# Second block's attention: two partition halves in one item, score products in turn, value products turned round

## The chip, the cores and the metric

One Trainium2 chip, and of its eight cores one. The metric is the device time of one execution of the program in microseconds; the kernel before ran three times for it, and one further execution was taken by the hardware profiler.

## The reference, cut to what matters

Two blocks of two layers each work on 256 tokens of width 1024. The change touches the attention of the second block, which each of its two layers computes twice: once with a window and a sink (kind 0 in the kernel, two shared key and value heads), once causal over one block of 256 keys (kind 1, eight heads each for q, k and v).

```python
HEAD_DIM = 64
def hybrid_layer_2(x, c, positions, ...):
    h = adaln(rms_norm(x, g_mix), sh1, sc1)
    proj = h @ w_in
    q_a, k_a, v_a, q_b, k_b, v_b, gate_a, gate_b = jnp.split(proj, IN_OFFSETS, axis=-1)
    ...
    y_a = swa_attention(q_a, k_a, v_a, sinks) @ w_o_swa
    y_b = moba_attention(q_b, k_b, v_b) @ w_o_moba
    mixed = jax.nn.sigmoid(gate_a) * y_a + jax.nn.sigmoid(gate_b) * y_b
    x = x + gt1[:, None, :] * (mixed @ w_out)

def swa_attention(q, k, v, sinks):
    s = einsum(q, k) * HEAD_DIM ** -0.5        # window of 128 keys: a query block of 128 sees at most 256
    p = softmax(concatenate([where(valid, s, NEG_INF), sink]))[..., :-1]
    return einsum(p, v)

def moba_attention(q, k, v):                   # 256 tokens are one block, so its own block is all there is
    ...
    s_own = where(kpos <= qpos, einsum(qc, k_own) * scale, NEG_INF)
    return einsum(softmax(s_own), v_own)
```

## The kernel before, in words

All large products are streams of weight tiles. A tile of 128 x 1024 float32 comes by DMA, ScalarE rounds it to a high part (`w<-w` on ACT), VectorE makes the low part as the difference (`w<-w,w` on DVE), and TensorE does three products a tile and output: high by high, high by low, low by high, in the one-pass format fp32r. A tile of a product with token rows out is twelve matmuls of 512 columns (`mm<-w,h`), one with features out twenty-four of 256 (`mm<-h,w`). At most three tiles are split ahead of TensorE.

Everything else is written as items: generators that issue a few instructions and yield what they wait for. A planner keeps a model of each engine's time (`Planner.note` adds the cost of each instruction) and decides after each weight step which item goes on, so the order on each engine comes out of that model. Attention items run in four lanes; a lane has two 128 x 512 tiles, named a and b (`l0a`, `l0b`, ... , and `vb` twice for the fourth lane), and a tile of small columns (`ls`). Four PSUM banks named p are shared by all items.

An attention item before is `group(t, hg)`: query block `t` of 128 tokens, and heads of one parity `e_`, whose q and k lie in partitions 0 to 63 or 64 to 127 of `qk`. For `t` = 0 there are two groups of four heads with 128 keys, for `t` = 1 four groups of two heads with 256 keys, so six a kind. A group does: score products with 64 rows of contraction into one bank (`p<-s`, 64*128 in the profile), mask add, row maximum, exponentials with their sums on ScalarE, four transposes (`p<-cst,l0a` and so on), a copy back to the lane's tile b, value products with the weights of the attention as the stationary side (128 x 128) and 64 columns of v moving (`p<-s,l1b` and so on), and a multiplication by the reciprocal of the sum into a tile `av`. When the groups of a block `t` are done, `outp` transposes `av` four times (`p<-cst,s`) and splits the result into high and low parts in `oo`. These attention products are plain float32 and stand in the profile as two records each; a transpose is one.

Kind 0 is set going when the third weight group of a layer's projections (q of kind 1) is done, and runs beside the products for k and v of kind 1; kind 1 follows beside the four gate products, and `oo` is used after those.

Of the kernel before, what the change touches and what calls it, by code (L numbers as in the profile page):

```python
# [7 lines left out]
F32 = mybir.dt.float32  # L8
F32R = mybir.dt.float32r
I32 = mybir.dt.int32  # L10
AF = mybir.ActivationFunctionType
# [74 lines left out]
class Planner:  # L86
# [46 lines left out]
    def note(self, eng, op, args, kw):  # L133
# [7 lines left out]
        if eng == PE:  # L141
# [441 lines left out]
def _build(tc, a, out, es):  # L583
# [22 lines left out]

    def LS(lane):

        t = sm.tile([128, 20], F32, name=f"ls{lane}", tag=f"ls{lane}")
        off = [0]  # L610

        def take(n):
            off[0] += n
            return t[:, off[0] - n:off[0]]
        return take
# [1351 lines left out]
        yield [sc2]  # L1967
        yield from rows2(0)

    def attend_items(kind, qk, vv, oo, avs, scol, need):  # L1970
        def group(t, hg, av):
            def gen(lane):
                yield [plan.after(g) for g in need]
                msk, rw, sc_ = B["msk"], B["rw"], LS(lane)
                nk = t + 1
                hpb = 4 // nk
                n = 128 * nk
# [3 lines left out]
                e_, p0 = hg % 2, hpb * (hg // 2)  # L1981
                gs_ = [2 * (p0 + i) + e_ for i in range(hpb)]
                gsl = slice(gs_[0], gs_[-1] + 1, 2)
                rr = slice(64 * e_, 64 * e_ + 64)
# [9 lines left out]
                sv = s.rearrange("p (h n) -> p h n", n=n)  # L1994
                nc.vector.tensor_tensor(sv, Sv, mk, ALU.add)
                plan.release(S)
                yield [s]
                mx = sc_(4)[:, 0:hpb]
                nc.vector.tensor_reduce(mx, sv, AX.X, ALU.max)
                yield [mx]  # L2000
                cs = scol[kind, t][:, gsl]
                sk, nsk = (b[:, gs_[0]:gs_[-1] + 1:2] for b in (rw[:, 256:264], B["nsk"]))
                nb = sc_(4)[:, 0:hpb]
                nc.vector.scalar_tensor_tensor(nb, mx, -1.0, cs, ALU.mult, ALU.mult)
                yield [nb]
                if kind == 0:
                    nc.vector.tensor_tensor(nb, nb, nsk, ALU.min)
                    yield [nb]
                    es_ = sc_(4)[:, 0:hpb]
                    nc.vector.tensor_tensor(es_, sk, nb, ALU.add)  # L2010
                den = sc_(4)[:, 0:hpb]
                for i in range(hpb):
                    nc.scalar.activation(sv[:, i, :], sv[:, i, :], AF.Exp, bias=nb[:, i:i + 1], scale=cs[:, i:i + 1],
                                         accum_out=den[:, i:i + 1])
                if kind == 0:
                    nc.scalar.activation(es_, es_, AF.Exp)
                yield [s, den]
# [12 lines left out]
                for i in range(hpb):  # L2030
                    g = gs_[i]
                    vo = 128 + 64 * g if kind else 64 * (g % 2)
                    for k in range(nk):
                        b = i * nk + k
# [4 lines left out]
                if kind:  # L2039
                    d = av.rearrange("p (h e d) -> p e h d", e=2, d=64)[:, e_, p0:p0 + hpb, :]  # L2040
                else:
                    d = av.rearrange("p (e h d) -> p e h d", e=2, d=64)[:, e_, p0:p0 + hpb, :]
                nc.vector.tensor_tensor(d, o_[:, 0:64 * hpb].rearrange("p (h d) -> p h d", d=64),
                                        rd.unsqueeze(2).to_broadcast([128, hpb, 64]), ALU.mult)
                plan.release(o_)
            return gen

        def outp(t, av, name):
            def gen(_):
                yield [plan.after(name)]  # L2050
                pt = yield Bank(av)
                transposes(pt, av, 4)
                yield [pt]
                ts = slice(128 * t, 128 * t + 128)
                yield from split(oo[:, kind, 0, :, ts], oo[:, kind, 1, :, ts], pt.rearrange("p (i n) -> p i n", n=128))
                plan.release(pt)
            return gen
        for t in range(2):
            name = f"att{kind}{t}"
            for hg in range(2 * (t + 1)):  # L2060
                plan.add(name, group(t, hg, avs(t)))
            plan.add(f"att{kind}", outp(t, avs(t), name), kind="pri")

    def residual(gt, c, X, sv, on_token):
        cs = slice(512 * c, 512 * c + 512)
# [14 lines left out]
    def layer2(l, X, norm, begin_next, on_token):  # L2080
# [7 lines left out]
        def pre_a():  # L2088
            st["qk"] = slot("s2", [128, 16, 256])
            t = slot("s3", [128, 4096])  # L2090
            st["vv"] = t[:, 0:1280].rearrange("p (t n) -> p t n", t=2)
            st["av"] = t[:, 1280:3328].rearrange("p (i n) -> p i n", i=4)

        def trans(qr, nb, dst, t):
            pt = yield Bank(qr)
# [26 lines left out]
        def attend(kind):  # L2122
            if not kind:
                if not l:
                    stream.gone()
                st["oo"] = slot("s4", [128, 2, 2, 4, 256], F32R)
            attend_items(kind, st["qk"], st["vv"], st["oo"], lambda t: st["av"][:, 2 * kind + t, :], scol,
                         (f"qk{kind}",))
# [294 lines left out]
```

## Time and profile before

| what | us |
|---|---|
| three runs | 2275.04, 2276.93, 2282.97 |
| median | 2276.93 |
| profiled execution, its own time | 2281.12 |
| its span, first to last instruction | 2278.6 |
| TensorE busy in the span | 2235.9 |
| VectorE, ScalarE, GpSimd busy | 1491.5, 1108.1, 268.7 |

The span is what the trace's rows add up to; the profiled execution's own time has 2.5 us around it. A busy TensorE is one with some matmul in flight, and since matmuls overlap, what a matmul costs is read from the distance between the starts of neighbours, not from its duration.

### The profile page before, as it was taken

What the parts mean: (1) busy time and instruction counts of PE and PEld (TensorE: products, weight loads), DVE (VectorE), ACT (ScalarE), POOL (GpSimd) and SP (SyncE); (2) the same over time, 40 slices, a digit from 0 to 9 for tenths busy, and PEclk for the clock granted to TensorE, in tenths of its full rate; (3) what the DMA queues carried; (4) which work ended last, traced back from release to release, by engine and by line L of the source; (5) the groups of instructions that cost most, each with busy time, mean ns of one, the idle gap of its engine ahead of it and who ended that gap; (6) DMA issues with size and microseconds to landing.
All of it is one profiled execution on the core that took longest, in us unless ns stands there. A gap on an engine that the chain in (4) does not pass through costs nothing. (4 is left out here: it accounts for less than half of the span.)

```text
span 2278.6 us, 34907 instructions
## 1 busy us (share of the span) xinstructions
PE 2235.9 (98%) x13192; PEld 1894.9 (83%) x13192; DVE 1491.5 (65%) x2868; ACT 1108.1 (49%) x2140; POOL 268.7 (12%) x451
## 2 busy tenths in 40 slices
PE   8999999999999999999999999999999999999999
PEld 6877888877777877878898888997998987798987
DVE  4767745567676635676885867678666656758554
ACT  4345323245465423435543566556655645656653
POOL 1013000033121000110200332002000002100000
PEclk9999999999999999999999999999999999999999
DMA  7443443443323454365683423464354564346454
GB/s 296 147 156 103 138 158 130 153 162 102 111 93 103 152 180 142 134 204 175 224 277 134 153 88 121 162 206 148 103 193 161 185 212 158 111 140 211 151 193 148
DMA packets 99912, 359.84 MB, mean 158 GB/s; under 512 B 11960, under 2 KB 12272, under 8 KB 99744
## 3 DMA queue, kind: packets, MB, share of 16 engines
q1 hardware_dynamic: 96192, 348.34, 45.6%
q0 software_dynamic: 3552, 9.28, 1.6%
q8 instruction: 103, 1.69, 0.3%
q14 instruction: 65, 0.53, 0.1%
HBM read 354.37 MB, written 3.20 MB: 157 GB/s over the span
## 5 line engine op out<-in xcount | busy, mean ns | idle before, releaser
L318 PE MATMUL mm<-h,w 128*128 128x256 f32 (+1 forms) x4048 | 819.7, 320 | 2.1 <-ACT qr L318 1.0
L318 DVE TENSOR_TENSOR w<-w,w 128x1024 fp32r<-128x1024 f32 x452 | 552.7, 1223 | 391.0 <-ACT w L318 340.8
L318 ACT ACTIVATE w<-w 128x1024 fp32r<-128x1024 f32 x461 | 486.4, 1058 | 661.9 <-PE mm L318 605.2
L318 PEld LDWEIGHTS mm<-h,w 128*128 128x128 f32 x4048 | 602.8, 190 | 61.6 <-issue 13.8
L318 PE MATMUL mm<-w,h 128*128 128x512 f32 (+1 forms) x1584 | 474.4, 394 | 10.8 <-DVE w L318 7.6
L318 PE MATMUL mm<-hl,w 128*128 128x512 f32 (+1 forms) x1040 | 354.2, 341 | 0.0
L318 PEld LDWEIGHTS mm<-w,h 128*128 128x128 f32 x1584 | 287.6, 191 | 79.8 <-DVE w L318 12.1
L318 PE MATMUL mm<-s,w 128*128 128x256 f32 (+1 forms) x1536 | 254.1, 325 | 1.1 <-DVE s L318 0.6
L318 PEld LDWEIGHTS mm<-s,w 128*128 128x128 f32 x1536 | 223.1, 190 | 25.3 <-issue 3.2
L318 PE MATMUL mm<-w,s 128*128 128x512 f32 x996 | 240.1, 391 | 0.0
L318 PE MATMUL mm<-w,hl 128*128 128x512 f32 (+1 forms) x608 | 232.9, 383 | 0.0
L318 PEld LDWEIGHTS mm<-w,s 128*128 128x128 f32 x996 | 186.2, 188 | 38.5 <-issue 0.4
L318 PEld LDWEIGHTS mm<-hl,w 128*128 128x128 f32 x1040 | 197.4, 190 | 20.8 <-issue 2.9
L318 DVE SCALAR_TENSOR_TENSOR acc<-w,stat,acc 128x512 f32<-128x512 f32 x192 | 143.8, 749 | 44.6 <-DMA w<-in_wada_dram 37.7
L318 PEld LDWEIGHTS mm<-w,hl 128*128 128x128 f32 x608 | 115.7, 190 | 22.6 <-DVE hl L318 0.2
L318 ACT ACTIVATE s<-mm 128x512 f32<-128x512 f32 (+2 forms) x142 | 67.2, 480 | 63.9 <-PE mm L318 63.7
L318 PE MATMUL p<-s 64*128 64x256 f32 (+3 forms) x464 | 85.8, 390 | 3.0 <-DVE s L318 1.5
L318 POOL TENSOR_TENSOR qrs<-qrs,mhalf 128x8 f32<-128x8 f32 (+2 forms) x48 | 80.2, 1672 | 4.0
L318 POOL TENSOR_SCALAR ls<-ls 128x1 f32<-128x1 f32 x72 | 25.9, 360 | 398.3 <-ACT l0a L318 124.7
L318 PE MATMUL mm<-s,s 128*128 128x512 f32 x252 | 67.8, 390 | 0.0
L318 PEld LDWEIGHTS p<-s 64*128 64x128 f32 (+1 forms) x464 | 47.0, 186 | 23.5 <-issue 6.3
L318 DVE TENSOR_REDUCE ls<-p 128x1 f32<-128x512 f32 (+1 forms) x96 | 52.9, 594 | 12.4 <-PE p L318 12.2
(314 smaller groups left out, 2422.2 us busy)
## 6 DMA issues: line engine op xcount, KB each, us to landing
w<-in_win_dram SPq DMA_DIRECT2D x272, 512.0 KB, 3.5
w<-in_wada_dram SPq DMA_DIRECT2D x144, 512.0 KB, 3.8
w<-in_wmix_dram SPq DMA_DIRECT2D x64, 512.0 KB, 3.6
w<-in_wup_dram SPq DMA_DIRECT2D x64, 512.0 KB, 3.7
w<-in_wdn_dram SPq DMA_DIRECT2D x64, 512.0 KB, 4.3
w<-in_wo_dram SPq DMA_DIRECT2D x16, 512.0 KB, 3.5
w<-in_wout_dram SPq DMA_DIRECT2D x16, 512.0 KB, 3.7
s<-in_x_dram SPq DMA_DIRECT2D x4, 512.0 KB, 8.0
```

What stands on the lines that cost most here:

```text
L318: r = f(*a, **k)
```

## The change

An item is now `group(t, p0)` and holds both partition halves: one item a kind for `t` = 0 (eight heads), two for `t` = 1 (four heads each), so three a kind in place of six. It takes two banks at once and issues its score products in turn, one of the lower and one of the upper half. It uses tiles a and b of its lane for the two halves, and small columns of eight, with the sink's term in columns of its own. The weights of the attention are multiplied by the reciprocal before they are transposed (two VectorE operations of 512 columns an item), the transposed weights go back into the same tiles, and the value products are turned round: v is the stationary side (128 rows, 64 columns), the weights move with 128 columns, and the two products of a pair write partitions 0 to 63 and 64 to 127 of one bank. The result lies as `oo` wants it, so `av` and `outp` go. The planner counts a matmul with 64 rows out, and a float32 one with 64 rows of contraction, at half.

```diff
-            if not f32 and ins[0].shape[0] == 64:
+            if ins[0].shape[0] == 64 or out.shape[0] == 64:
                 c /= 2
...
-        t = sm.tile([128, 20], F32, name=f"ls{lane}", tag=f"ls{lane}")
+        t = sm.tile([128, 24], F32, name=f"ls{lane}", tag=f"ls{lane}")
...
-                S = yield Bank(qk)
-                Sv = S.rearrange("p (h n) -> p h n", n=n)
+                gsl = slice(2 * p0, 2 * p0 + 2 * hpb)
+                heads = lambda x, e: x[:, e::2]
+                S = yield Bank(qk, n=2)
                 for i in range(hpb):
-                    g = gs_[i]
-                    kk = 12 if kind == 0 else 8 + g // 2
-                    nc.tensor.matmul(Sv[:, i, :], qk[rr, 4 * kind + g // 2, 128 * t:128 * t + 128], qk[rr, kk, 0:n],
-                                     start=True, stop=True)
-                yield [S]
-                s = LT(lane, "a")
...
+                    for e in range(2):
+                        rr = slice(64 * e, 64 * e + 64)
+                        kk = 12 if kind == 0 else 8 + p0 + i
+                        nc.tensor.matmul(S[e][:, n * i:n * i + n], qk[rr, 4 * kind + p0 + i, 128 * t:128 * t + 128],
+                                         qk[rr, kk, 0:n], start=True, stop=True)
+                yield S
+                s = [LT(lane, w) for w in "ab"]
...
-                rd = sc_(4)[:, 0:hpb]
-                nc.vector.reciprocal(rd, den)
-                pt = yield Bank(s)
-                transposes(pt, s, 4)
-                yield [pt]
-                wt = LT(lane, "b")
-                nc.scalar.activation(wt, pt, AF.Copy)
-                plan.release(pt)
-                o_ = yield Bank(wt)
...
-                        nc.tensor.matmul(o_[:, 64 * i:64 * i + 64], wt[:, 128 * b:128 * b + 128], vv[:, k, vo:vo + 64],
-                                         start=(k == 0), stop=(k == nk - 1))
+                nc.vector.reciprocal(den, den)
+                for e in range(2):
+                    yield [den]
+                    nc.vector.tensor_tensor(sv[e], sv[e], heads(den, e).unsqueeze(2).to_broadcast([128, hpb, n]), ALU.mult)
+                for e in range(2):
+                    pt = yield Bank(s[e])
+                    transposes(pt, s[e], 4)
+                    yield [pt]
+                    nc.scalar.activation(s[e], pt, AF.Copy)
+                    plan.release(pt)
+                o_ = yield Bank(*s)
+
+                if kind:
+                    visits = [(i, [(e, i) for e in range(2)]) for i in range(hpb)]
+                else:
+                    visits = [(e * hpb // 2 + i, [(e, 2 * i + m) for m in range(2)]) for i in range(hpb // 2)
+                              for e in range(2)]
+                for blk, pair in visits:
                     for k in range(nk):
...
+                        for m, (e, i) in enumerate(pair):
+                            vo = 128 + 64 * (2 * (p0 + i) + e) if kind else 64 * e
+                            b = i * nk + k
+                            nc.tensor.matmul(o_[64 * m:64 * m + 64, 128 * blk:128 * blk + 128], vv[:, k, vo:vo + 64],
+                                             s[e][:, 128 * b:128 * b + 128], start=(k == 0), stop=(k == nk - 1))
                 yield [o_]
...
-                nc.vector.tensor_tensor(d, o_[:, 0:64 * hpb].rearrange("p (h d) -> p h d", d=64),
-                                        rd.unsqueeze(2).to_broadcast([128, hpb, 64]), ALU.mult)
+                ts = slice(128 * t, 128 * t + 128)
+                ks = slice(p0, p0 + hpb) if kind else slice(p0 // 2, 4, 2) if t else slice(0, 4)
+                yield from split(oo[:, kind, 0, ks, ts], oo[:, kind, 1, ks, ts],
+                                 o_[:, 0:128 * hpb].rearrange("p (i n) -> p i n", n=128))
...
-        def outp(t, av, name):
-            def gen(_):
-                yield [plan.after(name)]
-                pt = yield Bank(av)
-                transposes(pt, av, 4)
```

The order on TensorE where the first score products of the first layer stand (`s_14757` is `qk`; `-` is the kernel before, `+` the changed one):

```order
 L318 MATMUL mm<-w_15068,h 128x512
-L318 MATMUL p_15110<-s_14757 128x128 x4
+L318 MATMUL p_15110<-s_14757 128x128
+L318 MATMUL p_15111<-s_14757 128x128
+L318 MATMUL p_15110<-s_14757 128x128
+L318 MATMUL p_15111<-s_14757 128x128
+L318 MATMUL p_15110<-s_14757 128x128
+L318 MATMUL p_15111<-s_14757 128x128
+L318 MATMUL p_15110<-s_14757 128x128
+L318 MATMUL p_15111<-s_14757 128x128
 L318 MATMUL mm<-w_15068,h 128x512
```

The four products of the second group, which stood one half tile further down, have moved up between the first four, and the two banks alternate.

TensorE in the kernel before, kind 0 of the same layer, between the fifth and the sixth tile after those scores (`s_14758` holds v):

```order
L318 MATMUL p_15314<-cst,l2a 128x128 x4
L318 MATMUL p_15321<-cst,vb_15234 128x128 x4
L318 MATMUL p_15332<-cst,l0a 128x128 x4
L318 MATMUL p_15341<-s_14758,l1b 128x64 x4
L318 MATMUL p_15359<-s_14757 128x256 x2
L318 MATMUL p_15365<-s_14758,l2b 128x64 x4
L318 MATMUL p_15370<-s_14758,vb_15328 128x64 x4
L318 MATMUL mm<-w_15296,h 128x512
```

and in the changed kernel the value products and a transpose of the same kind and layer:

```order
L318 MATMUL p_15552<-l2a,s_14758 64x128 x4
L318 MATMUL p_15552<-l2b,s_14758 64x128 x4
L318 MATMUL p_15562<-cst,vb_15307 128x128 x4
L318 MATMUL p_15570<-s_14757 128x256
L318 MATMUL p_15571<-s_14757 128x256
L318 MATMUL p_15570<-s_14757 128x256
L318 MATMUL p_15571<-s_14757 128x256
L318 MATMUL mm<-h,w_15500 128x256 x2
```

The transposes and value products of kind 0, which stood beside the products for v of kind 1 (`mm<-w,h`), now stand beside the first gate product (`mm<-h,w`), eight to eleven tiles after the first scores; the output has 64 rows and 128 columns.

VectorE of the changed kernel in the second layer, five to six weight tiles after the first scores (`w_18863` and `w_18918` are low parts of weight tiles, `vb` are score tiles of one item, `qr`, `g` and `ssq` belong to the projections):

```order
L318 TENSOR_TENSOR w_18863<-w_18684,w_18849 128x1024
L318 TENSOR_TENSOR g<-qr,hl 128x512
L318 TENSOR_TENSOR qr<-qr,hl 128x512
L318 TENSOR_TENSOR qr<-qr,g 128x512
L318 TENSOR_REDUCE ssq<-g 128x8
L318 TENSOR_TENSOR vb_18907<-p_18811,hl 128x512
L318 TENSOR_TENSOR vb_18908<-p_18812,hl 128x512
L318 SCALAR_TENSOR_TENSOR ls_18728<-ls_18728,scol 128x4
L318 TENSOR_TENSOR qr<-qr,qrs 128x512
L318 TENSOR_TENSOR g<-qr,hl 128x512
L318 TENSOR_TENSOR qr<-qr,hl 128x512
L318 TENSOR_TENSOR w_18918<-w_18735,w_18883 128x1024
```

Before, the fullest stretch between two low parts there held eight operations of 512 columns, one of 256 and eight small ones; now it holds nine of 512 and one small one. TensorE's order is the same outside the stretches with attention, but for eight transposes that move by a few matmuls; SyncE's and GpSimd's are the same throughout.

## Rows read from the trace of the kernel before

**Rows 1.** The page, busy time of each engine: us, share of the span, instructions.

```profile
PE 2235.9 (98%) x13192; PEld 1894.9 (83%) x13192; DVE 1491.5 (65%) x2868; ACT 1108.1 (49%) x2140; POOL 268.7 (12%) x451
```

**Rows 2.** Windows: length, busy (count) of PE, PEld, DVE, ACT, POOL, PEclk, DMA.

```profile
1573.00:1661.00 88.00, 87.00 (x605) 77.61 (x605) 59.46 (x119) 56.27 (x128) 9.77 (x10) 1.00 0.35 114
```

**Rows 3.** Groups by shape, TensorE, 1573 to 1661: count, busy us, mean ns, idle before.

```profile
L318 PE MATMUL p<-s 64*128 64x256 f32 x32 | 7.9, 402 | 0.5 <-DVE s L318 0.5
...
L318 PE MATMUL p<-s,l2b 128*128 128x64 f32 x24 | 3.3, 279 | 0.0
...
L318 PE MATMUL p<-cst,s 128*128 128x128 f32 x16 | 2.4, 272 | 0.0
```

**Rows 4.** Timeline of TensorE, score products: start us, length us, records, idle before.

```profile
1574.72 1.16 PE L318 MATMUL p<-s 64*128 64x128 f32 x8
1575.81 1.66 PE L318 MATMUL mm<-w,h 128*128 128x512 f32 x6
...
1581.87 1.14 PE L318 MATMUL p<-s 64*128 64x256 f32 x8
1582.94 0.96 PE L318 MATMUL mm<-w,h 128*128 128x512 f32 x3
```

**Rows 5.** Timeline of TensorE, value products and transposes after them.

```profile
1598.48 1.13 PE L318 MATMUL p<-s 64*128 64x256 f32 x4 [0.52 <-DVE s L318]
1599.54 1.10 PE L318 MATMUL p<-s,l2b 128*128 128x64 f32 x8
1600.48 1.06 PE L318 MATMUL p<-s,vb 128*128 128x64 f32 x8
1601.35 3.02 PE L318 MATMUL mm<-w,h 128*128 128x512 f32 x12
1604.21 0.60 PE L318 MATMUL p<-cst,s 128*128 128x128 f32 x4
1604.57 0.71 PE L318 MATMUL mm<-w,h 128*128 128x512 f32 x2
```

**Rows 6.** Timeline of TensorE, four column groups of 32 at a time.

```profile
1312.98 0.43 PE L318 MATMUL p<-acc,one 128*32 128x128 f32 x8
1313.34 0.39 PE L318 MATMUL mm<-h,w 128*128 128x256 f32 x1
```

**Rows 7.** Timeline of VectorE, second layer, where kind 0 begins.

```profile
1938.28 1.23 DVE L318 TENSOR_TENSOR w<-w,w 128x1024 fp32r<-128x1024 f32 x1 [1.50 <-ACT w L318]
1940.07 0.69 DVE L318 TENSOR_REDUCE ssq<-g 128x8 f32<-128x512 f32 x1 [0.56 <-ACT g L318]
...
1942.86 1.22 DVE L318 TENSOR_TENSOR w<-w,w 128x1024 fp32r<-128x1024 f32 x1
1943.99 0.68 DVE L318 TENSOR_REDUCE ssq<-g 128x8 f32<-128x512 f32 x1
1944.59 0.68 DVE L318 TENSOR_TENSOR vb<-p,hl 128x512 f32<-128x512 f32 x1
```

**Rows 8.** Timeline of TensorE at the same place.

```profile
1941.39 1.16 PE L318 MATMUL p<-s 64*128 64x128 f32 x8
```

**Rows 9.** Timeline of VectorE, second layer, waits behind TensorE.

```profile
1957.41 0.42 DVE L318 TENSOR_TENSOR s<-p,ls 128x256 f32<-128x256 f32 x1 [0.99 <-PE p L318]
...
1961.29 0.69 DVE L318 TENSOR_TENSOR vb<-p,hl 128x512 f32<-128x512 f32 x1 [1.12 <-PE p L318]
```

**Rows 10.** Timeline of TensorE, waits for a weight tile's low part.

```profile
1018.17 0.50 PE L318 MATMUL mm<-w,h 128*128 128x512 f32 x1 [1.77 <-DVE w L318]
...
1590.30 0.97 PE L318 MATMUL mm<-w,h 128*128 128x512 f32 x3 [0.48 <-DVE w L318]
...
1964.49 2.07 PE L318 MATMUL mm<-w,h 128*128 128x512 f32 x4 [2.43 <-DVE w L318]
```

**Rows 11.** Windows behind two of these waits, columns as in rows 2.

```profile
1018.00:1032.00 14.00, 13.83 (x45) 9.49 (x46) 4.47 (x13) 1.78 (x2) 0.00 (x0) 0.53 0.25 91
...
1964.50:1968.00 3.50, 3.50 (x9) 2.78 (x10) 3.50 (x8) 0.12 (x1) 0.00 (x0) 0.53 0.11 15
```

More of the change, by code (lines that the diff above doesn't have):

```diff
@@ L1968, in setup2, with attend_items, group @@
         yield from rows2(0)
-    def attend_items(kind, qk, vv, oo, avs, scol, need):
-        def group(t, hg, av):
+    def attend_items(kind, qk, vv, oo, scol, need):
+        def group(t, p0):
+            nk = t + 1
+            hpb = 4 // nk
+            n = 128 * nk
             def gen(lane):
@@ new lines, in gen @@
+                yield S
+                s = [LT(lane, w) for w in "ab"]
+                sv = [x.rearrange("p (h n) -> p h n", n=n) for x in s]
+                for e in range(2):
+                    nc.vector.tensor_tensor(sv[e], S[e].rearrange("p (h n) -> p h n", n=n), mk, ALU.add)
+                    plan.release(S[e])
+                    yield []
+                mx = sc_(2 * hpb)
+                for e in range(2):
+                    yield [s[e]]
+                    nc.vector.tensor_reduce(heads(mx, e), sv[e], AX.X, ALU.max)
@@ L2000, in gen @@
                 yield [mx]
-                cs = scol[kind, t][:, gsl]
-                sk, nsk = (b[:, gs_[0]:gs_[-1] + 1:2] for b in (rw[:, 256:264], B["nsk"]))
-                nb = sc_(4)[:, 0:hpb]
+                cs, sk, nsk = scol[kind, t][:, gsl], rw[:, 256:264][:, gsl], B["nsk"][:, gsl]
+                nb = mx
                 nc.vector.scalar_tensor_tensor(nb, mx, -1.0, cs, ALU.mult, ALU.mult)
@@ L2008, in gen @@
                     yield [nb]
-                    es_ = sc_(4)[:, 0:hpb]
+                    es_ = sc_(2 * hpb)
                     nc.vector.tensor_tensor(es_, sk, nb, ALU.add)
[L2011 to L2014, printed above, removed]
+                den = sc_(2 * hpb)
+                for e in range(2):
+                    for i in range(hpb):
+                        if i % 2 == 0 and (e or i):
+                            yield []
+                        g = slice(2 * i + e, 2 * i + e + 1)
+                        nc.scalar.activation(sv[e][:, i, :], sv[e][:, i, :], AF.Exp, bias=nb[:, g], scale=cs[:, g],
+                                             accum_out=den[:, g])
                 if kind == 0:
                     nc.scalar.activation(es_, es_, AF.Exp)
-                yield [s, den]
+                yield s + [den]
                 if kind == 0:
@@ L2020, in gen @@
                     yield [den]
-                rd = sc_(4)[:, 0:hpb]
-                nc.vector.reciprocal(rd, den)
-                pt = yield Bank(s)
-                transposes(pt, s, 4)
-                yield [pt]
-                wt = LT(lane, "b")
-                nc.scalar.activation(wt, pt, AF.Copy)
-                plan.release(pt)
-                o_ = yield Bank(wt)
-                for i in range(hpb):
-                    g = gs_[i]
-                    vo = 128 + 64 * g if kind else 64 * (g % 2)
-                    for k in range(nk):
-                        b = i * nk + k
-                        nc.tensor.matmul(o_[:, 64 * i:64 * i + 64], wt[:, 128 * b:128 * b + 128], vv[:, k, vo:vo + 64],
-                                         start=(k == 0), stop=(k == nk - 1))
@@ L2037, in gen @@
-                yield [o_]
[L2039 to L2042, printed above, removed]
-                nc.vector.tensor_tensor(d, o_[:, 0:64 * hpb].rearrange("p (h d) -> p h d", d=64),
-                                        rd.unsqueeze(2).to_broadcast([128, hpb, 64]), ALU.mult)
+                nc.vector.reciprocal(den, den)
@@ new lines, in gen @@
+                for e in range(2):
+                    yield [den]
+                    nc.vector.tensor_tensor(sv[e], sv[e], heads(den, e).unsqueeze(2).to_broadcast([128, hpb, n]), ALU.mult)
+                for e in range(2):
+                    pt = yield Bank(s[e])
[9 more added lines that the diff above has]
+                              for e in range(2)]
@@ L2058, in attend_items @@
         for t in range(2):
[L2059 to L2062, printed above, removed]
+            for p0 in range(0, 4, 4 // (t + 1)):
+                plan.add(f"att{kind}", group(t, p0))
     def residual(gt, c, X, sv, on_token):
@@ L2126, in attend @@
                 st["oo"] = slot("s4", [128, 2, 2, 4, 256], F32R)
-            attend_items(kind, st["qk"], st["vv"], st["oo"], lambda t: st["av"][:, 2 * kind + t, :], scol,
-                         (f"qk{kind}",))
+            attend_items(kind, st["qk"], st["vv"], st["oo"], scol, (f"qk{kind}",))
         gemm(lambda q: win[l, 0, q], 8, 512, toks, ev_q(0), need=("rows",), pre=pre_a, tneed=norm.tneed(lambda o: [o]), head=EXT)
```

19 lines of the change are left out of this document (removed).

## The prediction

> **What bounds the kernel now.** I read the page first: TensorE is busy for 98% of the span [rows 1], so a microsecond of TensorE work taken away is one gained, unless TensorE then waits. The change touches only the second block's attention, some 90 us in each of its two layers. In the window of the first of them TensorE is busy for 87.0 of 88 us and VectorE for 59.5 [rows 2]. So VectorE has room over the whole stage, but not everywhere: the timeline shows TensorE stopped there for 0.52 us behind a score product's operand [rows 5] and for 0.48 us behind the low part of a weight tile, and in the second layer for 2.43 us behind a low part [rows 10]. After that last wait the granted clock was 0.53 over 3.5 us, the lower level of 1.2 GHz for nearly all of it [rows 11]; at full clock this work takes 0.47 x 3.5 = 1.6 us less. These waits cost 0.5 + 0.5 + 2.4 + 1.6 = 5.0 us in the two layers.
>
> **TensorE's work, part by part.** Costs are distances between the starts of neighbouring rows.
>
> Score products: a group of four narrow ones is eight records and takes 1575.81 - 1574.72 = 1.09 us; a group of two wide ones is four records and takes 1599.54 - 1598.48 = 1.06 us [rows 4, 5]. But where the planner happened to put a lower and an upper wide group beside each other with their records alternating, both together, eight records, took 1582.94 - 1581.87 = 1.07 us [rows 4]. So alternating halves run at the same time. The order of before holds 8 narrow groups and 16 wide ones, six of these in three such pairs: 8 x 1.09 + 10 x 1.06 + 3 x 1.07 = 22.5 us. Afterwards all alternate, in 4 narrow and 8 wide blocks: 4 x 1.09 + 8 x 1.07 = 12.9 us. That is 9.6 us less. For narrow ones the trace shows no clean pair; if they did not overlap, the four blocks would take twice the time and 4.4 us of this would be lost. I take full overlap, as the wide row has it.
>
> Value products: a group's four are eight records of 64 columns and take 0.87 to 0.94 us [rows 5], 0.11 us a record; 24 groups (four names of 24 records each in a layer [rows 3]) make 24 x 0.9 = 21.6 us. Turned round there are eight an item, sixteen records of 128 columns. The nearest row to two column halves is one with four column groups: eight records, two waves of four, took 1313.34 - 1312.98 = 0.36 us with the change back to the full array in it [rows 6]. A record alone takes 0.11 us and eight would take 0.9, so column groups overlap too. Eight waves of two at 0.11 and some 0.15 for the two changes of shape are 1.05 us an item, 12.6 us for twelve: 9.0 us less. The bounds: without overlap 16 x 0.11 + 0.15 = 1.9 us, 22.9 in all, 1.3 us more than now; with no price for the changes of shape 10.8. The row is on the side of overlap, and I take 9.0.
>
> The Trainium skill, TensorEngine Tiling (Array Packing), Performance Considerations, recommends just this for a moving side of 64 or fewer columns, swapping the two sides and tiling columns, for a factor of two. By that factor the value products would come to 10.8 us, and the sum would be 1.8 us better.
>
> The transposes of `outp` go: eight times four, at 1604.57 - 1604.21 = 0.36 us [rows 5], sixteen records a layer [rows 3]: 2.9 us. The transposes of the weights stay as many.
>
> Together 9.6 + 9.0 + 2.9 = 21.5 us of TensorE work.
>
> **The other engines.** VectorE gains two multiplications of 512 columns an item. Such an operation lasts 0.68 us and its neighbour follows after 0.60 [rows 7]; with some that wait for their own predecessor I count 0.62, so 24 x 0.62 = 15 us. It loses the final multiplications, 8 of 256 columns (0.42 us long [rows 9], some 0.34 apart) and 16 of 128 (half as many columns, an estimate of 0.2): 6 us, and some 40 small operations at 0.1 us: 4 us. Net 5 us more over two stages in which it is idle for 28 us each [rows 2]. Nothing hides it if it falls where VectorE is behind; then it costs up to 5 us. ScalarE has the same exponentials and copies.
>
> **What is late next.** All that attention work leaves TensorE's queue, but the low parts stay on VectorE's, and a tile has only 12 x 0.23 = 2.75 us of products. I counted the order of the changed kernel in the second layer from the low part that is in use when the first scores come, to the seventh low part after it. TensorE has 7 tiles, three score blocks (3.2) and three times four transposes of projections (1.3): 23.8 us. VectorE has 29 operations of 512 columns at 0.62, seven low parts at 1.13 [rows 7] and five small ones: 26.4 us. The lead at the start is that of before: the low part ended at 1938.28 + 1.23 = 1939.51 and TensorE came to it five matmuls and a switch ahead of its scores at 1941.39, at 1940.16 [rows 7, 8], 0.65 us. So TensorE has to wait 26.4 - 23.8 - 0.65 = 2.0 us in the second layer. The same count in the first, to the eighth low part, gives 27.2 against 26.5 us: with the same lead no wait. VectorE waits itself too; for a square that ScalarE makes it was 0.56 us [rows 7], which I add once a layer, 0.6. So waits of 0.6 and 2.6 us. The large one is long enough that the clock may fall as it did after 2.43 us, and after 1.77 us in the first block, where it was 0.53 over 14 us, a loss of 6.6 [rows 10, 11]. Between 0 and 6.6 I take 3. After: 0.6 + 2.6 + 3.0 = 6.2 us against 5.0 before. The later stretch, kind 1 beside the gate products, carries the transposes and value products that moved down, and there TensorE has more to do than VectorE.
>
> **The sum.** 21.5 - 1.2 = 20.3 us less. The profiled execution's own time was 2281.1 us, 2.5 of it outside the span and untouched: 2260.8. The median of the three runs shown is 4.2 us lower, so on its scale 2256.6; I say 2257.
>
> **The rivals.**
> VectorE sets the pace (2 in 10). Its waits for results of TensorE, 0.99 and 1.12 us behind value and score products [rows 9], made it fall behind in the second layer before: by the same count TensorE had 21.4 and VectorE 20.1 us of work up to the low part that came 2.43 us late, so that about 4.4 us of waiting must have been its own, and 1.5 in the first layer. If as much stays, the waits become 1.5 and 6.4 us, with clock losses of 1.6 and 6.6: 16.1 against 5.0, the gain shrinks to 10.4 and the time is 2266. Against it: in the changed order the score adds of that stretch stand well behind their products, and no value product is waited for there.
> The Trainium skill, same page and section, warns that tiling speeds up TensorE but not the emptying of PSUM, which may then be the limit; this rival is the form that the warning would take here.
> The column halves do not overlap (1 in 12). Then the value products get 1.3 us dearer instead of 9.0 cheaper, the gain is 10, and the time 2267. Rows 6 speak against it.
> The kernel gets slower (1 in 40) if TensorE's waits for low parts repeat tile after tile and hold the clock at its lower level. Each microsecond there loses 0.47; the gain is used up at 20.3 / 0.47 = 43 us more at the lower level, about three stretches as long as the longest seen [rows 11]. With half of both stages at it, 80 us, it would lose 38 and end near 2294. For it speaks that VectorE's count is above TensorE's in that stretch; against it that the shortage is over after some eight tiles.
> That nothing happens, since the halves overlapped anyway, is excluded for 18 of 24 groups by the order; what is left of it is two mishaps at once, 1 in 40.
>
> **How the numbers follow.** My forecast has 7 chances in 10. Its own range is from waits and clock losses that vanish (26.5 us less, 2250) to 2262. With VectorE's rival and the column one the range goes up to 2267; two or three in a hundred at the lower end are left out by starting at 2251. What a measurement of this kernel can tell from no change is about 0.3%, 6.8 us. Nearly all of the forecast and most of both rivals lie beyond that: faster 0.93, the same 0.04, slower 0.03.
>
> **What would show it.** Right: score blocks of eight wide or sixteen narrow records in 1.07 to 1.09 us; value blocks of sixteen records in about 1.05; no `p<-cst,s`; each attention stage some 10 us shorter; a wait for a low part of 2 to 3 us in the second layer's kind 0, and a dip of the clock behind it. Wrong: value blocks near 1.9 us; waits for low parts in the first layer beyond 1 us; clock at the lower level for more than 15 us in a stage; or VectorE idle where TensorE waits, which would mean that the order and not the work is late.

## The result, and the profile after

The changed kernel took 2255.26 us (median of four runs, 2254.68 to 2256.68) against 2277.47 us before: a ratio of 0.990, with an interval of 0.9881 to 0.9919, 22 us less. Measured again beside the experiments it took 2258.82 us (six runs, 2254.06 to 2267.11) against 2277.28; why these scatter more is told below. The profiled execution took 2254.68 us, with a span of 2252.9.

The page, busy time of each engine, and windows of the first attention stage and behind the wait of 1.7 us in the first block (columns as in [rows 1] and [rows 2]):

```profile
PE 2207.0 (98%) x13160; PEld 1868.6 (83%) x13160; DVE 1493.1 (66%) x2830; ACT 1107.5 (49%) x2138; POOL 270.5 (12%) x451
```

```profile
1566.00:1652.00 86.00, 84.12 (x651) 74.39 (x651) 63.87 (x104) 60.45 (x133) 9.83 (x10) 1.00 0.42 133
1018.00:1032.00 14.00, 13.71 (x70) 10.52 (x71) 6.57 (x16) 3.70 (x5) 0.00 (x0) 1.00 0.51 173
```

TensorE's total fell by 28.9 us, with 32 instructions less, while VectorE's rose by 1.6. In the stage VectorE is busy for 63.9 of 86 us, where it was 59.5 of 88 [rows 2]. The second row answers to the first of [rows 11]: at the same place the granted clock is now 1.00.

TensorE's timeline of the changed kernel, columns as in [rows 4], with a block of narrow scores, one of wide scores and one of value products, each with the row that ends it:

```profile
1567.96 1.16 PE L318 MATMUL p<-s 64*128 64x128 f32 x16
1569.06 1.66 PE L318 MATMUL mm<-w,h 128*128 128x512 f32 x6
...
1573.83 1.14 PE L318 MATMUL p<-s 64*128 64x256 f32 x8
1574.89 3.01 PE L318 MATMUL mm<-w,h 128*128 128x512 f32 x12
...
1613.32 1.09 PE L318 MATMUL p<-vb,s 128*64 128x128 f32 x16
1614.34 1.93 PE L318 MATMUL mm<-h,w 128*128 128x256 f32 x14
```

Sixteen narrow records take 1569.06 - 1567.96 = 1.10 us, eight wide ones 1.06, sixteen value records 1.02. All three are what the forecast had (1.09, 1.07, 1.05).

The waits of TensorE in the two stages, from the same timeline:

```profile
1589.00 2.81 PE L318 MATMUL mm<-w,h 128*128 128x512 f32 x11 [0.92 <-DVE w L318]
...
1596.46 2.53 PE L318 MATMUL mm<-h,w 128*128 128x256 f32 x19 [0.84 <-DVE w L318]
...
1946.38 0.63 PE L318 MATMUL p<-cst,qr 128*128 128x128 f32 x4 [1.36 <-DVE qr L318]
...
1948.75 5.83 PE L318 MATMUL mm<-w,h 128*128 128x512 f32 x23 [1.51 <-DVE w L318]
...
1955.72 4.46 PE L318 MATMUL mm<-h,w 128*128 128x256 f32 x35 [0.47 <-DVE w L318]
...
1983.39 2.90 PE L318 MATMUL mm<-h,w 128*128 128x256 f32 x22 [1.02 <-DVE w L318]
1990.40 1.34 PE L318 MATMUL mm<-h,w 128*128 128x256 f32 x9 [0.38 <-ACT s L318]
```

With one of 0.1 us they come to 6.6 us, against 3.4 before [rows 5, 10]. The table adds up the distances between the starts of TensorE's records over both stages, waits of over 0.1 us taken out:

| both layers, us | before | changed | difference | forecast |
|---|---|---|---|---|
| score products | 21.93 | 12.68 | -9.25 | -9.6 |
| value products | 20.55 | 11.84 | -8.71 | -9.0 |
| transposes of `outp` | 3.16 | 0 | -3.16 | -2.9 |
| other transposes | 12.73 | 12.91 | +0.18 | 0 |
| waits | 3.43 | 6.62 | +3.2 | -0.2 |
| lower clock | 1.6 | 0 | -1.6 | +1.4 |

The sum is -19.3. Measured from a weight tile's low part ahead of a stage to the same one behind it, the first layer's stage went from 122.64 to 113.12 us and the second's from 123.38 to 113.94: 19.0 us less. The two spans differ by 25.7. Of the other 6.7 us, 6.0 lie in the first block, which the change does not touch: around 1018 us both kernels wait for a low part, 1.77 us before [rows 10] and 1.71 after, and only in the profiled execution of before did the clock fall behind it.

```profile
1018.29 0.50 PE L318 MATMUL mm<-w,h 128*128 128x512 f32 x1 [1.71 <-DVE w L318]
```

### The profile page after: what moved, and what is told of

Same layout as the page of the kernel before. It is cut to its first block, busy times and chain, and to the rows that moved or that the text cites. A ratio compares the mean times of both kernels' runs of the same rounds, so it can differ in the third digit from the quotient of the medians.

```text
span 2252.9 us, 34811 instructions
## 1 busy us (share of the span) xinstructions
PE 2207.0 (98%) x13160; PEld 1868.6 (83%) x13160; DVE 1493.1 (66%) x2830; ACT 1107.5 (49%) x2138; POOL 270.5 (12%) x451
## 5 line engine op out<-in xcount | busy, mean ns | idle before, releaser
L318 PE MATMUL mm<-w,h 128*128 128x512 f32 (+1 forms) x1584 | 467.9, 390 | 9.7 <-DVE w L318 6.6
L318 PEld LDWEIGHTS mm<-s,w 128*128 128x128 f32 x1536 | 223.1, 190 | 25.7 <-issue 3.2
L318 PE MATMUL p<-s 64*128 64x256 f32 (+3 forms) x464 | 75.9, 389 | 2.5 <-ACT l1b L318 1.1
L318 PEld LDWEIGHTS p<-s 64*128 64x128 f32 (+1 forms) x464 | 40.4, 186 | 21.4 <-issue 6.5
```

The costliest lines, as they stand in the source:

```text
L318: r = f(*a, **k)
```

## The experiments

All times are medians beside runs of the kernel before on the same chip, which lay between 2276.7 and 2277.3 us. Times of different groups of experiments are set beside each other with care; the profiles decide.

### What makes the halves overlap

**Score products half by half.**

```diff
-                for i in range(hpb):
-                    for e in range(2):
+                for e in range(2):
+                    for i in range(hpb):
```

> The changed kernel with the score products of an item issued half by half: all of the lower half, then all of the upper. Theory 1, the halves run at the same time only where their records alternate: score blocks take 2.1 to 2.2 us in place of 1.07, 9.3 us more of TensorE's work in the two layers; up to 3 us of it fills waits for low parts beside kind 0, so 6 to 9.5 us more, 2261 to 2265. Theory 2, the order inside a block does not matter: blocks stay at 1.07 us and the time within 1.5 us of 2255.

Measured: 2261.75 us (2258.34 to 2264.79), ratio 0.993 (0.9917 to 0.9943). TensorE's timeline of this kernel:

```profile
1570.84 1.71 PE L318 MATMUL p<-s 64*128 64x128 f32 x16
1572.48 0.72 PE L318 MATMUL mm<-w,h 128*128 128x512 f32 x2
...
1577.25 1.14 PE L318 MATMUL p<-s 64*128 64x256 f32 x8
1578.32 3.01 PE L318 MATMUL mm<-w,h 128*128 128x512 f32 x12
```

Neither theory held. A narrow block takes 1.64 us, between 1.1 and 2.2; a wide one 1.07, as with turns. Score products cost 15.12 in place of 12.68 us in the two layers, only 2.4 us more. The median lies where theory 1 had it, but the 9.3 us of work behind that did not come: in the profiled execution both stages together were 3.8 us longer than in the changed kernel, and behind the long waits of the second layer the granted clock was 0.83 over 1950 to 1960 us, where it had been 1.00.

**Value products half by half.**

```diff
-                for blk, pair in visits:
-                    for k in range(nk):
-                        for m, (e, i) in enumerate(pair):
+                for m in range(2):
+                    for blk, pair in visits:
+                        for k in range(nk):
+                            e, i = pair[m]
```

> The changed kernel with the value products of an item issued column half by column half. Theory 1, column halves overlap only between neighbours: blocks of sixteen records take 1.85 to 1.9 us in place of about 1.0, 10 us more in the two layers, little of it hidden since the blocks stand beside the gate products where TensorE has more to do than VectorE: 2262 to 2266. Theory 2, the gain comes from turning the product round and not from neighbours: blocks stay near 1.0 us and the time within 1.5 us of 2255.

Measured: 2263.11 us (2261.51 to 2264.49), ratio 0.9936 (0.9924 to 0.9948). Value products took 16.57 in place of 11.84 us, 4.7 us more; a block on average about 1.4 us, between the theories. Here too the median is in theory 1's range with half of its work: both stages were 7.1 us longer, 4.7 of it these blocks, and the clock was 0.66 over 1950 to 1960 us. TensorE's timeline, where the program issues four records of `l2a` and four of `l2b` for the lower column half and then the same for the upper:

```profile
1612.39 0.65 PE L318 MATMUL p<-l2a,s 128*64 128x128 f32 x4
1612.87 0.27 PE L318 MATMUL p<-l2b,s 128*64 128x128 f32 x1
1612.88 0.32 PE L318 MATMUL p<-l2a,s 128*64 128x128 f32 x1
1612.98 0.27 PE L318 MATMUL p<-l2b,s 128*64 128x128 f32 x1
1613.04 0.27 PE L318 MATMUL p<-l2a,s 128*64 128x128 f32 x1
...
1613.37 0.60 PE L318 MATMUL p<-l2b,s 128*64 128x128 f32 x4
```

The upper half's first `l2a` starts at 1612.88, ahead of three records of `l2b` that the program issues before it. So TensorE does not wait with the other half until its turn comes: it starts it beside the fifth record of the first half instead of behind the eighth, four records early, runs both side by side, and ends with the last four of the upper half alone. That is why wide blocks, with four records a half, lose nothing. The Trainium skill, TensorE: Matmul & The Clock Gate, The mechanism, says that matmuls start and end strictly in program order and that only weight loads are pulled ahead. The rows above disagree, for matmuls in different column halves; the measurement decides.

**Halves kept apart.** Half by half as in the two runs before, and with a wait between the halves of an item, so that weight products come between.

```diff
+                    if e:
+                        yield [S[0]]
...
+                    if m:
+                        yield [o_]
```

> The changed kernel with the halves of an item's score products and of its value products separated by a wait, so that weight products stand between them. Theory 1, TensorE starts the other half while the first is still being issued, about four records ahead, so halves overlap wherever they stand next to each other in its queue, and not when other work stands between: score products cost some 9 us and value products some 9 us more in the two layers, time 2268 to 2274. Theory 2, turning and pairing are worth something on their own (shorter records): less than half of that, under 2264.

Measured: 2282.24 us (2279.4 to 2288.26), ratio 1.0023 (1.0013 to 1.0033): slower than the kernel before. TensorE's timeline:

```profile
1617.84 1.16 PE L318 MATMUL p<-s 64*128 64x128 f32 x8
1618.93 0.63 PE L318 MATMUL mm<-h,w 128*128 128x256 f32 x3
...
1620.57 1.09 PE L318 MATMUL p<-vb,s 128*64 128x128 f32 x8
1621.59 0.63 PE L318 MATMUL mm<-h,w 128*128 128x256 f32 x3
```

Half a block alone takes 1.09 us (scores) and 1.02 us (values), as long as the whole block of the changed kernel. Scores came to 22.65 us and value products to 24.13, 10.0 and 12.3 more: more than theory 1 had, and for the value products 3.6 us more than in their old orientation. So the whole gain of both hangs on the other half being next in TensorE's queue. Putting both halves into one item gives that; taking turns adds 2.4 and 4.7 us of it. Turning the product round is a loss by itself.

### Where the waits come from

**The changed kernel again.**

> The changed kernel once more, unaltered, beside the others on the same chip. Theory 1, it is a steady 2255 us: median within 1.5 us of 2255.3, and what scores and values by half cost beyond their blocks (6.5 and 7.8 us against 1.9 and 4.7 us of TensorE's work) came with them. Theory 2, executions scatter by lower granted clock at the long waits: median up to 2259, and a profile with a clock below 1 somewhere after 1946 us would be no surprise.

Measured: 2258.82 us (2254.06 to 2267.11), ratio 0.9919 (0.99 to 0.9937): theory 2. (The 1.9 us in the expectation left some records out; over all of them it is the 2.4 above.) The window of 1950 to 1960 us in the first execution of the changed kernel:

```profile
1950.00:1960.00 10.00, 9.53 (x60) 8.17 (x59) 8.08 (x19) 9.77 (x25) 0.00 (x0) 1.00 0.39 116
```

and the same window and a row of TensorE's timeline in this one:

```profile
1950.00:1960.00 10.00, 9.53 (x34) 7.58 (x35) 5.78 (x14) 6.61 (x17) 0.00 (x0) 0.71 0.22 63
```

```profile
1950.00 8.26 PE L318 MATMUL mm<-w,h 128*128 128x512 f32 x23 [1.51 <-DVE w L318]
```

The same 23 matmuls behind the same wait of 1.51 us took 8.26 us here and 5.83 above. The program, the order and the waits are the same; the granted clock is not. The stage is 116.37 us long in place of 113.94.

**No normalisation**: the multiplication by the reciprocal left out.

```diff
-                for e in range(2):
-                    yield [den]
-                    nc.vector.tensor_tensor(sv[e], sv[e], heads(den, e)..., ALU.mult)
```

> The changed kernel without the multiplication of the attention weights by the reciprocal (left out altogether, 24 VectorE operations of 512 columns). Theory 1, these 15 us of VectorE are what TensorE waits for in the two stages: the waits there fall from 6.5 to 2 us or less, the time by 4 to 5 us to 2250 or 2251. Theory 2, the waits come from VectorE waiting for other engines and from the order: they fall by less than 1.5 us and the time stays at 2254 to 2255.

Measured: 2253.36 us (2251.84 to 2254.25), ratio 0.9893 (0.988 to 0.9906). The waits fell to 4.3 us: those of 0.84, 0.47, 1.02 and 0.38 went, while 0.92, 1.36 and 1.51 stayed (one of 0.36 for ScalarE came). The two stages together were 1.7 us shorter. Between the theories: without the 24 operations 2.3 of the 6.6 us are gone, the later waits, not the first ones; since the planner's order moves too, how much of this is their work and how much the order is not told apart.

**The normalisation on GpSimd.**

```diff
-                    nc.vector.tensor_tensor(sv[e], ...
+                    nc.gpsimd.tensor_tensor(sv[e], ...
```

> The changed kernel with the multiplication by the reciprocal on GpSimd. Theory 1, VectorE's work is what is late: as without the multiplication, 3 to 5 us less, 2250 to 2252, if GpSimd takes up to about 1.5 us for 512 columns, since an item then only ends later. Theory 2, GpSimd is slow at it (3 us or more) or VectorE's operations lengthen beyond 0.68 us beside it: no gain, 2255 to 2259.

Measured: 2258.3 us (2257.14 to 2261.16), ratio 0.9917 (0.9904 to 0.993). GpSimd's timeline, and then VectorE's:

```profile
1600.15 2.02 POOL L318 TENSOR_TENSOR l1b<-l1b,ls 128x512 f32<-128x512 f32 x1
1602.55 1.04 POOL L318 TENSOR_TENSOR l2a<-l2a,ls 128x512 f32<-128x512 f32 x1 [0.38 <-DVE ls L318]
```

```profile
1602.95 1.72 DVE L318 TENSOR_TENSOR w<-w,w 128x1024 fp32r<-128x1024 f32 x1 [0.49 <-ACT w L318]
```

GpSimd takes 1.04 to 2.06 us for 512 columns, and a low part beside it 1.72 in place of 1.22 us. Not every low part lengthens: one at 1621.22 us took 1.23, and there the operation of GpSimd beside it was the one of 2.06. TensorE waits for GpSimd (0.59 and 0.88 us in the first layer) as well as for low parts; the waits come to 7.7 us. Theory 2. The Trainium skill, GPSIMD Engine Reference, Key points, names the contention with VectorE operations that read two inputs from SBUF; the longer low parts agree.

**No rotation for kind 1**: its sine part left out.

```diff
-...B["SW"][:, t, i, :])], k0, use)
+...B["SW"][:, t, i, :] if i < 2 else None)], k0, use)
```

> The changed kernel without the sine part of the rotation of kind 1's q and k (left out: two VectorE operations of 512 columns a projection tile, 8 a layer, just ahead of and beside kind 0's first attention items). Theory 1, VectorE's load in that stretch is what TensorE waits for: the waits for low parts there (0.92 and 0.84 us in the first layer, 1.36, 1.51 and 0.47 in the second) fall to under 1.5 us in all, time 2250 to 2252. Theory 2, VectorE waits there for ScalarE's squares and exponentials: the waits stay within 1 us of 5.1 and the time at 2254 to 2256.

Measured: 2256.43 us (2255.87 to 2258.88), ratio 0.9905 (0.9891 to 0.9918). TensorE's timeline in the second layer:

```profile
1941.59 3.04 PE L318 MATMUL mm<-w,h 128*128 128x512 f32 x12 [0.92 <-DVE w L318]
1946.38 3.06 PE L318 MATMUL mm<-w,h 128*128 128x512 f32 x12 [1.75 <-DVE w L318]
1950.03 1.20 PE L318 MATMUL mm<-w,h 128*128 128x512 f32 x4 [0.59 <-DVE w L318]
```

With eight operations of VectorE a layer gone, the waits came to 7.7 us, not to less. Theory 1 falls: it is not the sum of VectorE's work alone. Theory 2 is nearer, with more waits and half a microsecond more time than it had; its cause was looked for in VectorE's own timeline of the changed kernel:

```profile
1587.72 1.23 DVE L318 TENSOR_TENSOR w<-w,w 128x1024 fp32r<-128x1024 f32 x1 [1.12 <-PE mm L318]
...
1954.44 1.23 DVE L318 TENSOR_TENSOR w<-w,w 128x1024 fp32r<-128x1024 f32 x1 [1.78 <-ACT s L318]
...
1982.11 1.23 DVE L318 TENSOR_TENSOR w<-w,w 128x1024 fp32r<-128x1024 f32 x1 [2.13 <-ACT l1b L318]
```

Three of the low parts for which TensorE waits (at 1589.00, 1955.72 and 1983.39) stand behind idle time of VectorE itself, of 1.1 to 2.1 us. The ScalarE operations that the last two rows name did not end it. In the trace's semaphore events VectorE went on each time 0.04 us after TensorE's semaphore rose at the end of a weight product (1587.64, 1954.36 and 1982.03 us), when the rounding of the tile had been done for at least 0.5 us and its DMA for over 10. So VectorE waited for TensorE, and TensorE then waited for the low part. A low part reads nothing that TensorE makes, so it was probably waiting for the buffer that it writes, one of the nine tile buffers of the weight stream; that is read from the kernel, and no run varied it. Ahead of the waits of 0.84, 1.36 and 1.51 us VectorE was busy. Without the rotation VectorE's idle time ahead of such a low part grew to 5.34 us, ended by a weight product as well, and TensorE's wait behind it stayed at 0.92 us in each layer:

```profile
1581.61 1.23 DVE L318 TENSOR_TENSOR w<-w,w 128x1024 fp32r<-128x1024 f32 x1 [5.34 <-PE mm L318]
```

**Kind 0 set going later.**

```diff
-        do(lambda: attend(0))
         gemm(lambda q: win[l, 2, q], 8, 512, toks, ev_k)
+        do(lambda: attend(0))
```

> The changed kernel with kind 0's attention set going after the k products of kind 1 instead of before them, so that it no longer stands beside the rotations. Theory 1, VectorE's load in the stretch of both is what is late: the 5.1 us of waits beside kind 0 fall to 1.5 or less and no others come, 2250 to 2252. Theory 2, the load only moves: as many us of waits turn up beside the v products and the first gate products, 2254 to 2257.

Measured: 2266.51 us (2264.83 to 2267.8), ratio 0.9947 (0.9935 to 0.9959), worse than both theories. TensorE's timeline, and ScalarE's ahead of the second wait:

```profile
1615.99 0.66 PE L318 MATMUL p<-cst,vb 128*128 128x128 f32 x4 [2.87 <-ACT l1a L318]
...
1979.68 1.65 PE L318 MATMUL mm<-h,w 128*128 128x256 f32 x6 [3.92 <-ACT s L318]
```

```profile
1978.79 0.57 ACT L318 ACTIVATE l2b<-p 128x512 f32<-128x512 f32 x1
1979.27 0.89 ACT L318 ACTIVATE s<-mm 128x256 f32<-128x256 f32 x3
```

The waits moved beside the gate products and grew to 10.9 us. There ScalarE works off the exponentials and four copies of transposed weights before it takes the gate results (`s<-mm`) out of PSUM. The clock fell behind both long waits (columns as in [rows 2]):

```profile
1617.30:1620.70 3.40, 3.40 (x25) 3.07 (x22) 1.54 (x2) 3.05 (x8) 0.00 (x0) 0.50 0.00 0
1979.68:1986.50 6.82, 6.82 (x47) 6.27 (x48) 2.59 (x7) 2.67 (x6) 0.00 (x0) 0.54 0.00 0
```

At full clock this work takes 0.50 x 3.4 + 0.46 x 6.8 = 4.8 us less. With the 4.3 us of added waits that is most of the 11.1 us by which both stages were longer than in the changed kernel, so the clock cost about as much as the waits themselves.

**The planner's three levers.** Other work held back sooner (`slack` at 0.5 us in place of `SLACK`, 1.2); the next tile's parts ahead of other work (`split` in front of `side` after each weight step), both from kind 0's start to kind 1's; and the changed line on costs undone.

```diff
-        if max(self.t[ACT], self.t[DVE]) < now + (SLACK if slack is None else slack):
+        if max(self.t[ACT], self.t[DVE]) < now + self.slack:
```

> The changed kernel with the planner holding back other work while VectorE or ScalarE is more than 0.5 us (in place of 1.2) ahead of TensorE in its model, from kind 0's start to kind 1's. Theory 1, the waits for low parts come from the planner, which fills VectorE with attention and rotation work up to that bound whatever there is, so that a low part stands behind it: the 5.1 us of waits beside kind 0 fall to under 2.5 us and the time to 2252 to 2254. Theory 2, VectorE's total work there is too much for any order: waits of the same size a few tiles later, 2255 to 2259.

```diff
                     self.dma()
+                    if plan.eager:
+                        self.split()
                     n = 0
```

> The changed kernel with the low and high part of the next weight tile issued ahead of other work after each weight step, from kind 0's start to kind 1's. Theory 1 (as for the lower bound): low parts come earlier, the waits for them beside kind 0 fall from 5.1 us to under 2.5, 2252 to 2254. Theory 2: the rest of VectorE's work is late in their place, and TensorE waits for rotated tiles (qr) or score tiles by as much: 2255 to 2259.

```diff
-            if ins[0].shape[0] == 64 or out.shape[0] == 64:
+            if not f32 and ins[0].shape[0] == 64:
```

> The changed kernel with the planner's line on costs as it was before, so that it counts score and value products at full price. Theory 1, the line only moves when items go on, which decides where waits fall: blocks as in the changed kernel (1.07, about 1.0 us), waits in the two stages between 4 and 10 us, time 2253 to 2260. Theory 2, it decides whether halves stand beside each other: blocks longer by more than 1 us in all, time over 2260.

Measured: 2259.53 us (2257.55 to 2259.84), 2255.76 (2252.72 to 2260.55) and 2261.3 (2258.97 to 2266.21); ratios 0.9921 (0.9909 to 0.9934), 0.9909 (0.9895 to 0.9922) and 0.9934 (0.9922 to 0.9947). TensorE's timeline of the first and of the second:

```profile
1591.33 2.83 PE L319 MATMUL mm<-w,h 128*128 128x512 f32 x11 [1.18 <-DVE w L319]
...
1596.08 0.66 PE L319 MATMUL p<-cst,qr 128*128 128x128 f32 x4 [1.49 <-DVE qr L319]
```

```profile
1597.78 2.51 PE L319 MATMUL mm<-h,w 128*128 128x256 f32 x13 [1.90 <-DVE w L319]
```

Holding back takes no waits away: 7.4 us of them, on other tiles; theory 2. Parts first splits the theories by layer: in the second layer the waits fell from 4.7 to 1.3 us, in the first they rose from 1.9 to 4.3. With the old costs blocks stay as they are (scores 13.0, values 12.0 us) and the waits come to 7.5 us, as theory 1 has it; the time is a little above it, in part since in its profiled execution the clock fell in the first block too.

**Parts first in the second layer alone.**

```diff
-        do(lambda: attend(0))
+        do(lambda: (setattr(plan, 'eager', l == 1), attend(0)))
```

> The changed kernel with low and high parts issued ahead of other work in the second layer alone, beside kind 0. Theory 1, in that layer low parts issued earlier do away with most of the 4.7 us of waits (1.3 us were left when both layers had it) and with the pair of long waits behind which the granted clock fell in some executions: own time of an undisturbed execution 2.4 us below that of the changed kernel, median 2252 to 2254, and no lower clock at 1950 us. Theory 2, the gain seen in that layer depended on what the first layer's order left behind, or was chance: 2255 to 2258.

Measured: 2252.1 us (2250.66 to 2254.57), ratio 0.9889 (0.9872 to 0.9905). TensorE's timeline in the second layer:

```profile
1951.59 3.12 PE L319 MATMUL mm<-h,w 128*128 128x256 f32 x24 [0.47 <-DVE w L319]
1955.39 1.82 PE L319 MATMUL mm<-h,w 128*128 128x256 f32 x13 [0.68 <-DVE w L319]
```

Theory 1. The pair of 1.36 and 1.51 us is gone, and 1.3 us of waits are left in this layer. From the first layer's marked low part to the end of the span it takes 689.4 us against 693.7 in the changed kernel. It is below both medians of the changed kernel, but the two were not timed together, so an interval between them is not to be had.

## Why the prediction was right, and where it was not

**Time.** 2257 stands between the two medians of 2255.3 and 2258.8. The change itself gave 19.0 us where 20.3 were forecast. The step from the profiled execution to the median was an offset of 4.2 us, without a cause. The likely cause is the first block's clock loss of 6.0 us, which some profiled executions have and some do not; the changed kernel's, at 2254.7 and not 2260.8, had none. The unprofiled runs scatter with the clock as well: of the 17 of the kernel before beside the second measurement, the three with a mean granted clock of 0.993 took 2280.96 to 2283.26 us and the three with 0.998 2273.74 to 2275.18. Where in the program it fell in them no trace shows.

**Score products, 9.6 forecast, 9.25 measured.** The size was right, its ground was not. "Alternating halves run at the same time" took the alternation in the trace for one in the program. In the kernel before each group was issued whole; TensorE itself had interleaved the records of [rows 4]. So the half-by-half theories, 2.1 us or 1.07, were both the wrong question. The statement that the trace shows no clean pair of narrow groups was also wrong, since the timeline of before holds one:

```profile
1616.27 1.71 PE L318 MATMUL p<-s 64*128 64x128 f32 x16
1617.91 0.62 PE L318 MATMUL mm<-h,w 128*128 128x256 f32 x3
```

Two narrow groups, issued one after the other, took 1.64 us and not 2 x 1.09. That is the 1.64 of the half-by-half run, and most of the half microsecond by which 22.5 stood above the measured 21.9.

**Value products, 9.0 and 8.7; `outp`, 2.9 and 3.2.** Both right (8 x 0.11 + 0.15 is 1.03 and not 1.05; the measured block is 1.02). The bound without overlap, 22.9 us, was reached and passed by the kernel with halves apart (24.1): 16 x 0.11 us held, but two half blocks also pay the changes of shape twice. The factor of two that the Trainium skill, TensorEngine Tiling (Array Packing), Performance Considerations, gives for the swap came out at 20.55 / 11.84 = 1.7.

**Waits, 3.2 forecast, 6.6 measured: the term that failed.** For the second layer's kind 0, up to the seventh low part, the count gave 2.6, and 1.36 + 1.51 = 2.9 came. What it had at next to nothing was the rest: 0.92 and 0.84 in the first layer and 0.47, 1.02 and 0.38 beside the gate products, "there TensorE has more to do than VectorE". Sums of work on two engines cannot see these. VectorE was idle ahead of three of those low parts (2.4 of the 6.6 us), the sign that the prediction had named for an order that is late; what it idled for was TensorE itself. The first layer's waits, 1.9 us in all though none over 1 us alone, touch another sign named there, waits beyond 1 us in that layer. Leaving the normalisation out took 2.3 us of waits and 1.7 us of time away, within the "up to 5 us" that was set aside and then counted as hidden. VectorE's own total was not the surprise: 5 us more were forecast, and it rose by 1.6.

**Clock, 3.0 forecast, 0 and 2.4 measured.** The forecast put a mean between two outcomes, which is what the two profiled executions show. That the waits were sized too small and the clock's loss too large hid both in the total, and that is luck.

**The rivals.** "VectorE sets the pace" had 1.5 and 6.4 us of waits; 1.9 and 4.7 came, nearer to it than to the forecast. Its mechanism, that VectorE falls behind by its own waits for TensorE, is half there: VectorE did wait for TensorE ahead of 2.4 us of the waits, but at the end of weight products and not for score or value results. The runs that took VectorE work away and still had 4.3 and 7.7 us of waits do not decide it: without the normalisation two of these three waits went, and without kind 1's rotation a wait of 0.92 us with VectorE idle ahead of it came in each layer. Its clock losses of 8.2 us did not come. "The column halves do not overlap" is refuted for neighbours and true for halves apart. That the kernel would get slower needed the lower clock for 43 us more; behind these waits the clock cost the changed kernel nothing in one profiled execution and 2.4 us in the other.

**What stays open.** Why the same rule of the planner helps in one layer and hurts in the other was not settled. Nor was it shown which buffer VectorE waited for ahead of 1589, 1955 and 1983 us, and whether one buffer more, or low parts written to another, would end these waits.

## What to carry to other kernels

Work for the two halves of the array overlaps if it stands next to each other in TensorE's queue, so build items that hold both halves; the order inside decides the rest, and strict turns are best. Turn a product round for column halves only where the pair stays together, since apart it is dearer than before. When an engine's total leaves room and another still waits for it, look for idle time of that engine ahead of the late instruction, and for what ended it, before taking work away from it.

## What the runs showed of the hardware

- TensorE started matmuls of the other row or column half about four records ahead of their place in the program: in the by-half runs blocks took 1.64 (narrow scores) and about 1.4 us (values), against 1.10 and 1.02 in turns and twice 1.09 and 1.02 with the halves apart.
- The clock behind one and the same wait is a matter of the execution. Around 1018 us all fourteen profiled executions waited 1.5 to 1.8 us for the same low part. In three the mean granted clock of 1019 to 1029 us was 0.50 to 0.59, which is the lower level of 1.2 GHz for most of it; in eleven it was 1.00. Longer waits were not the ones that fell: the clock fell behind 1.53 us in one execution and stayed behind 1.71 in another.
- GpSimd's elementwise operation of 512 columns varied from 1.04 to 2.06 us, and low parts of VectorE beside such operations took between 1.22 and 2.04 us, where 1.22 is their length alone.
